# One core, one decoder trunk: the order of the attention passes, a scaling on ScalarE, and the layout of the token factors

## The chip, the core and the metric

The kernel runs on one core of one Trainium2 chip. The core has a matrix engine (TensorE: PE for its matmuls, PEld for its weight loads), VectorE (DVE), ScalarE (ACT), GpSimd (POOL) and SyncE (SP), which here only issues DMAs. Each engine works through its own list of instructions in the order in which the program has them; semaphores tie the lists together. Matmuls write to PSUM, which has eight banks of 128 partitions by 512 fp32 columns; SBUF holds everything else on the core.

The metric is the device time of one execution in microseconds.

## The reference: what is computed

The input is a residual stream of 512 tokens by 1024 columns, fp32. Two layers follow: a gated short convolution, then sliding-window attention whose keys and values are computed once. Each is followed by a SwiGLU feed-forward network (FFN) of width 2816.

```python
kv = rmsnorm(h, kv_norm) @ w_kv                       # 4 K heads, 4 V heads of 64
q = partial_rotary((rmsnorm(h, b_pre_norm) @ b_w_q))  # 16 heads of 64, blocks of 128 tokens
scores = q @ concat(k_prev_block, k_block).T / 8      # masked to a window of 128
probs = softmax(concat([scores, sink]))[..., :-1]     # the sink takes a share and gives nothing
h = h + rmsnorm((probs @ v) @ b_w_o, b_post_norm)
g, u = split(rmsnorm(h, ffn_pre_norm) @ w_gate_up)    # in each layer
h = h + rmsnorm((silu(g) * u) @ w_down, ffn_post_norm)
```

## The kernel before, in words

**Numbers.** A matrix product is made from a rounded part and a rest: every fp32 operand is split into `hi` (rounded to the format that TensorE reads fast, written by ACT) and `lo` (what is left, written by DVE), and `mm3` (L190 to L193) sums lo by hi, hi by hi and hi by lo. All transposes run on TensorE against an identity.

**FFN.** Each FFN has 11 pairs of gate and up tiles; one pair is computed plainly, the other ten as blocks of two by two with seven products in place of eight (`gate_jobs`). Three of the seven products (6, 7 and 4) go to the chain "X", which collects in a bank of 512 columns. For these, the token factor's hi and lo stand in one buffer, so that one matmul over 512 columns (L1048) multiplies hi and lo by the weights' hi at once, and a second over 256 columns (L1050) adds hi by the weights' lo. The other products use `mm3` over 256 columns. The token factors are made once per FFN in `factors` (L364): a buffer `two` of 1024 columns has hi in its first 512 columns and lo in the last 512, for two values of k. The operand of L1048 for one k therefore is two runs of 256 columns, 512 columns apart. Weights stream in by DMA; for each product DVE may first add two of them (L457), ACT writes their hi (L469) and DVE their lo (L470), three products ahead of TensorE. POOL's queue issues DMAs that form sums of weights in memory.

**Attention.** The 16 heads go in eight pairs, t = 0 to 7. A loop makes ten passes, i = 0 to 9, and the string `ORDER` (L47) gives the order in which a pass writes its steps into the engines' lists. The steps are, with their heads' place in the software pipeline:

- S0, S1 `scores` (pair i): 12 matmuls each over two banks `psc`, for tokens 0 to 255 and 256 to 511
- M0, M1 `maxima` (pair i, DVE, L1311): adds the mask, finds the maxima, and so frees the banks `psc`; E00 to E11 `exponents` (ACT, L1327)
- N0, N1 `normalise` (pair i, DVE, L1339 to L1344): sums, a reciprocal, and four scalings of the tiles `s`, one per head and block of 128 tokens; for N0 the first block's tile is 128x128, the other 128x256
- T0 to T3 `turn` (pair i-1, PE, L1356): transposes of `s` into banks `pt`, of which there are two; P0 to P3 `high` (ACT, L1369) and L0 to L3 `low` (DVE, L1373) split them and so free the bank for T two later
- W0 to W3 `weigh` (pair i-1, PE): by the values, into `po`; O- `out` splits `po` in the pass behind (ACT L1390, DVE L1391)
- Q0 to Q3 `project` (pair i+2, PE): the queries, in quarters of 6 matmuls, into `pq`; R- `rotate` (pair i+1, DVE L1237 and L1239, then POOL L1240 and L1241); H- `split` (pair i+1, ACT L1246, then POOL L1247), whose result S0 of the next pass reads; G the next weights of the queries (ACT L186, DVE L187)
- K, in pass 2 alone: the second half of the keys, on DVE, POOL and ACT as R- and H-
- g, Z, z, A: first parts of the output projection, from pass 4 on, and the first weights of the FFN behind

A line in an engine's list waits only for what it reads and for the buffer it writes; what stands behind it on that engine waits as well. The PSUM banks `pq`, `po` and `pe` rotate through four, `psc` and `pt` through two each.

Of the kernel before, what the change touches and what calls it, by code (L numbers as in the profile page):

```python
# [12 lines left out]
AF = mybir.ActivationFunctionType  # L13
ALU = mybir.AluOpType
# [4 lines left out]
S = 512  # L19
# [24 lines left out]
LINE_LEAD = 3  # L44

EARLY_IN, REST_IN = 2, 0
ORDER = (  # L47
    "R- T0 g0 S0 O- T1 Q0 M0 Q1 Z0 P0 P1 S1 T2 L0 Q2 L1 G M1 E00 E01 T3 H- Q3 P2 P3 E10 E11 Z1 z0 K W0 L2 L3 A A A N0 W1 W2 N1 W3 g1 z1"
)
STEP = {  # L50
    "S": "scores", "M": "maxima", "E": "exponents", "N": "normalise", "T": "turn", "P": "high",
# [4 lines left out]
EARLY = 4  # L56
# [16 lines left out]
def yoco_kernel(  # L73
# [22 lines left out]
    nc = tc.nc  # L96
# [15 lines left out]
    def name(s):  # L112
        uid[0] += 1
        return f"{s}_{uid[0]}"
# [4 lines left out]
    def wide(s, dt=F32):  # L119
        return wides.tile([P, D], dt, tag="wide", name=name(s))  # L120
# [52 lines left out]
    def split_weights(src, raw=None, slots=False):  # L173
        if raw is None:
            raw = fetch(src)
        if slots:
            hi, lo = Two("whi", F32R), Two("wlo", F32R)
            for h in range(2):
                c = slice(h * S, (h + 1) * S)
                nc.scalar.activation(hi[:, c], raw[:, c], AF.Copy)  # L180
                nc.vector.tensor_tensor(out=lo[:, c], in0=raw[:, c], in1=hi[:, c].bitcast(F32),
                                        op=ALU.subtract)
            return hi, lo
        hi = wsp.tile([P, D], F32R, tag="whi", name=name("whi"))
        lo = wsp.tile([P, D], F32R, tag="wlo", name=name("wlo"))
        nc.scalar.activation(hi, raw, AF.Copy)  # L186
        nc.vector.tensor_tensor(out=lo, in0=raw, in1=hi.bitcast(F32), op=ALU.subtract)  # L187
        return hi, lo
# [50 lines left out]
    class Update:  # L239
# [124 lines left out]
        def factors(self):  # L364


            x = self.x[0]
            made = {p: [] for p in range(1, 8)}
            for p, k0, c in ((1, 0, 0), (2, 4, 0), (3, 4, 256)):
                made[p] = [[a[:, c : c + 256] for a in x[k0 + k]] for k in range(4)]  # L370
            for j in range(2):
                q11, q21, q12, q22 = (self.parts[i, hf, j] for hf in range(2) for i in range(2))

                nc.vector.tensor_tensor(out=q11, in0=q11, in1=q12, op=ALU.subtract)
                nc.vector.tensor_tensor(out=q12, in0=q22, in1=q12, op=ALU.subtract)
                nc.vector.scalar_tensor_tensor(out=q22, in0=q22, scalar=-1.0, in1=q11,
                                               op0=ALU.mult, op1=ALU.subtract)
                nc.vector.scalar_tensor_tensor(out=q21, in0=q22, scalar=-1.0, in1=q21,
                                               op0=ALU.mult, op1=ALU.subtract)
                for p, q in ((6, q22), (5, q11), (7, q12), (4, q21)):  # L380
                    two = wide("xt", F32R)
                    hi, lo = two[:, :S], two[:, S:]
                    two = two.rearrange("p (i c) -> p i c", i=2)
                    nc.scalar.activation(hi, q, AF.Copy)
                    nc.vector.tensor_tensor(out=lo, in0=q, in1=hi.bitcast(F32),
                                            op=ALU.subtract)
                    made[p] += [[hi[:, c : c + 256], lo[:, c : c + 256], two[:, :, c : c + 256]]
                                for c in (0, 256)]
            return made

    class Ahead:
# [156 lines left out]
    for l in range(2):  # L548
# [3 lines left out]
        for rd, (f0, f1) in enumerate(ROUNDS[:-1]):  # L552
            k = slice(f0 // 2, f1 // 2)
# [106 lines left out]
    with tc.manual_schedule(engines=ALL):  # L660
# [294 lines left out]
    def ffn(l, before, ahead, gain, gpres, following):  # L955
# [5 lines left out]
        def gate_pair(pg, pu):  # L961
# [12 lines left out]
            return pair_sums(gr, acts[0])  # L974

        def gate_jobs(q, factors, out, to, then):


# [256 lines left out]
    def rope(ps, eng):  # L1235
        sh = slot("sh")
        nc.vector.stream_shuffle(sh, ps, swap)  # L1237
        a = slot("ra")
        nc.vector.tensor_tensor(out=a, in0=ps, in1=ctab, op=ALU.mult)  # L1239
        eng.tensor_tensor(out=sh, in0=sh, in1=stab, op=ALU.mult)  # L1240
        eng.tensor_tensor(out=a, in0=a, in1=sh, op=ALU.add)  # L1241
        return a

    def rope_split(a, eng):
        hi, lo = slot("rhi", F32R), slot("rlo", F32R)
        nc.scalar.activation(hi, a, AF.Copy)  # L1246
        eng.tensor_tensor(out=lo, in0=a, in1=hi.bitcast(F32), op=ALU.subtract)  # L1247
        return hi, lo
# [24 lines left out]
    class Heads:  # L1273
# [62 lines left out]
        def normalise(self, half):  # L1336
            se, rs = self.sums[half]
            pe = self.pe[half]
            nc.vector.tensor_tensor(out=se, in0=se, in1=rs, op=ALU.add)  # L1339
            rd = small.tile([P, 2, 2], F32, tag="rd", name=name("rd"))  # L1340
            nc.vector.reciprocal(out=rd, in_=se)
            for i, cc in self.spans(half):
                for e in range(2):
                    nc.vector.tensor_scalar(  # L1344
                        out=pe[e][:, cc], in0=pe[e][:, cc], scalar1=rd[:, e, i : i + 1],
                        scalar2=None, op0=ALU.mult,
                    )

        def turn(self, j):
            pt = bank("pt", ps_pt)  # L1350
# [67 lines left out]
    with tc.manual_schedule(engines=ALL):  # L1418
        last_tile(res, [[(0, 4)], [(0, 5)], [], [(0, 6), (0, 7), (1, 0), (1, 1)],
                        [(1, f) for f in (4, 5, 2, 3, 6, 7)]])  # L1420
        for hf in range(2):
            c = slice(hf * 256, (hf + 1) * 256)
# [48 lines left out]
    with tc.manual_schedule(engines=ALL):  # L1471
        sum_on("a0")
        for i in range(KT + 2):
            if i == KT:
                res = Update(mix_o, B_ATT, [G_FPRE[1]])
                res.leaves = True
                ahead = Ahead(first_weights(1))
            if i == KT + 1:
                res.load()
            for c in ORDER.split():  # L1480
                if c == "A":
                    if i == KT:
                        ahead.one()
                    continue
                if c == "K":
                    if i == 2:
                        ks.append(rope_split(rope(pk[1], nc.gpsimd), nc.gpsimd))
                    continue
                late = c.endswith("-")
                op, n = c[0], [int(d) for d in c[1:].rstrip("-")]  # L1490
                t = i - late
                if op == "g":

                    u = 2 * (t - EARLY - 1) + n[0]
                    if u in (-2, -1, 2, 3):
                        j = u + 2 if u < 0 else u
                        early_w.append(split_weights(w_o[j // 2, j % 2], slots=j >= EARLY_IN))
                    continue
                if op in "SMENTPLWO":
                    t -= op in "TPLWO"  # L1500
                    of = hp
                elif op in "QRH":
                    t += LEAD
                    of = qs
                elif op == "G":
                    t += LEAD + 1
                    of = qs
                    if KT <= t < KT + 4:
                        j = t - KT
                        rest_w.append(split_weights(w_o[j // 2, 2 + j % 2], slots=j >= REST_IN))  # L1510
                else:
                    t = 2 * (t - EARLY - 1) + n.pop(0)
                    of = early
                if 0 <= t < len(of) and not (op in "RH" and t < LEAD - 1):
                    getattr(of[t], STEP[op])(*n)
                if op in "RH" and i <= KT:
                    issue(len(issues) // 2 if op == "R" else len(issues))
            if i <= KT:
                sum_on(f"a{i + 1}")
        close(rest_w, at, EARLY, res, ahead, lambda: sum_on(f"a{KT + 2}"), 1)  # L1520
# [96 lines left out]
```

## Time and profile before

| What | Value |
|---|---|
| median of 3 runs | 1026.7 us (1026.5 to 1026.81) |
| profiled execution, own time | 1026.46 us |
| its span on the core | 1024.7 us |
| PE busy | 1015.1 us, 6168 matmuls |
| DVE busy | 858.7 us, 1440 instructions |
| ACT busy | 582.3 us, 1035 instructions |
| POOL busy | 196.9 us, 259 instructions |
| granted TensorE clock, mean | 0.999 |
| DMA | 244.52 MB, mean 239 GB/s |

The span holds, in this order, the convolution layer, the first FFN (its blocks of two by two run from 209.7 us), the attention passes (550.6 to 661 us), and the second FFN (blocks from 715 us). A row of a timeline has start, duration, engine, line, operation, output<-input, shape, and the count of equal instructions merged into the row. A duration of a matmul is from issue to modelled end and overlaps the next one; how long one holds the engine is read from the distance of two starts.

### The profile page before, as it was taken

The page shows a single profiled execution, that of the slowest core. Times are in us where ns is not written, and L with a number is a line of the kernel's source. Part 1 is how long each engine was busy: PE and PEld are TensorE (multiplying, and loading weights), DVE is VectorE, ACT ScalarE, POOL GpSimd, SP SyncE. Part 2 cuts the span into 40 slices and gives each one's busy share as a digit, 9 for nine tenths or more (in the row PEclk, how much of TensorE's full clock was granted, in tenths as well). Part 3 has the DMA queues.
Part 4 walks back from the last instruction along what each step waited for, and adds up shares of the span by engine and source line. Part 5 has one row for each costly group of instructions (what it writes and reads, how often), then busy time and mean ns, then how long its engine had stood idle before and what let it go on. Part 6 is the DMA issues. An engine that isn't in the chain of part 4 may idle for free.

```text
span 1024.7 us, 16538 instructions
## 1 busy us (share of the span) xinstructions
PE 1015.1 (99%) x6168; PEld 900.3 (88%) x6168; DVE 858.7 (84%) x1440; ACT 582.3 (57%) x1035; POOL 196.9 (19%) x259
## 2 busy tenths in 40 slices
PE   9999999999999999999999999999999999999997
PEld 8888888999889898998897888889998998989986
DVE  5766767889789988989869998778997898889896
ACT  7323445865655454666476776677666554645641
POOL 0443033112111111000123653232111010110001
PEclk9999999999999999999999999999999999999999
DMA  9897689459979699879504779976899576998742
GB/s 357 288 266 225 184 255 350 136 167 292 348 238 296 195 305 307 267 210 318 170 5 160 187 229 277 254 264 153 270 289 328 167 245 226 299 298 249 240 149 82
DMA packets 66576, 244.52 MB, mean 239 GB/s; under 512 B 7872, under 2 KB 8384, under 8 KB 54720
## 3 DMA queue, kind: packets, MB, share of 16 engines
q1 hardware_dynamic: 51328, 145.98, 38.9%
q0 software_dynamic: 14592, 96.48, 36.9%
q8 instruction: 48, 0.79, 0.3%
q10 hardware_dynamic: 576, 1.02, 0.3%
q14 instruction: 32, 0.26, 0.1%
HBM read 237.15 MB, written 102.76 MB: 332 GB/s over the span
## 4 chain that ended last, share of the span: by engine, by line
PE 85%; DVE 8%; ACT 2%; DMA 2%; issue 2%; POOL 0%; DVEq 0%; ACTq 0%
PE gx L1048 10%; PE gx L1050 5%; PE pcub L191 4%; PE pcub L192 4%; PE pcub L193 4%; PE gz L193 3%; PE gz L192 3%; PE gz L191 3%; PE px L191 3%; PE px L193 3%; PE px L192 3%; PE pmix L191 2%; PE pmix L192 2%; PE pmix L193 2%; DMA raw<-in_w_gb_dram 2%; PE gy L193 2%
## 5 line engine op out<-in xcount | busy, mean ns | idle before, releaser
L470 DVE TENSOR_TENSOR wlo<-raw,whi 128x1024 fp32r<-128x1024 f32 x225 | 274.8, 1227 | 64.5 <-ACT whi L469 64.1
L469 ACT ACTIVATE whi<-raw 128x1024 fp32r<-128x1024 f32 x225 | 234.0, 1051 | 104.8 <-DVE raw L457 22.3
L1048 PE MATMUL gx<-xt,whi 128*128 128x512 f32 x480 | 172.5, 399 | 0.1
L1050 PE MATMUL gx<-xt,wlo 128*128 128x256 f32 x480 | 135.0, 281 | 0.0
L1048 PEld LDWEIGHTS gx<-xt,whi 128*128 128x128 f32 x480 | 90.4, 188 | 19.7 <-DVE st L1008 0.3
L538 POOL DMA_DIRECT2D hsum<-in_w_gb_dram x96 | 63.7, 751 | 143.9 <-ACT whi L469 82.6
L1050 PEld LDWEIGHTS gx<-xt,wlo 128*128 128x128 f32 x480 | 90.9, 189 | 0.1
L1024 ACT ACTIVATE st<-gx 128x256 f32<-128x256 f32 x120 | 43.0, 379 | 63.1 <-PE gx L1050 47.8
L538 POOL DMA_DIRECT2D hsum<-hsum x32 | 25.3, 790 | 258.9 <-ACT whi L469 192.0
L1008 DVE TENSOR_TENSOR st<-gx,st 128x256 f32<-128x256 f32 x160 | 62.9, 420 | 4.3 <-ACT st L1024 2.9
L192 PE MATMUL pcub<-xhi,whi 128*128 128x512 f32 x168 | 65.4, 389 | 0.0
L191 PE MATMUL pcub<-xlo,whi 128*128 128x512 f32 x168 | 65.4, 389 | 0.0
L193 PE MATMUL pcub<-xhi,wlo 128*128 128x512 f32 x168 | 65.4, 389 | 0.0
L1062 ACT ACTIVATE gr<-gr 128x1024 f32<-128x1024 f32 x20 | 21.3, 1065 | 49.2 <-DVE gr L1008 49.2
L191 PE MATMUL px<-wlo,ahi 128*128 128x512 f32 x120 | 46.8, 390 | 0.1
L192 PE MATMUL px<-whi,ahi 128*128 128x512 f32 x120 | 46.7, 389 | 0.0
L193 PE MATMUL px<-whi,alo 128*128 128x512 f32 x120 | 46.7, 389 | 0.0
L193 PE MATMUL gz<-xhi,wlo 128*128 128x256 f32 x160 | 45.4, 284 | 0.0
L191 PE MATMUL gy<-xlo,whi 128*128 128x256 f32 x160 | 45.3, 283 | 0.0
L192 PE MATMUL gy<-xhi,whi 128*128 128x256 f32 x160 | 45.3, 283 | 0.0
L193 PE MATMUL gy<-xhi,wlo 128*128 128x256 f32 x160 | 45.3, 283 | 0.0
L192 PE MATMUL gx<-xhi,whi 128*128 128x256 f32 x160 | 45.3, 283 | 0.0
(265 smaller groups left out, 3064.5 us busy)
## 6 DMA issues: line engine op xcount, KB each, us to landing
hsum<-in_w_gb_dram POOLq DMA_DIRECT2D x96, 512.0 KB, 7.9
raw<-hsum SPq DMA_DIRECT2D x88, 512.0 KB, 7.6
raw<-in_w_gb_dram SPq DMA_DIRECT2D x60, 512.0 KB, 7.6
hsum<-in_w_dn_dram POOLq DMA_DIRECT2D x36, 512.0 KB, 8.8
raw<-in_w_dn_dram SPq DMA_DIRECT2D x32, 512.0 KB, 6.0
hsum<-hsum POOLq DMA_DIRECT2D x28, 512.0 KB, 5.9
raw<-in_w_in_dram SPq DMA_DIRECT2D x21, 512.0 KB, 7.8
hsum<-in_w_dn_dram POOLq DMA_DIRECT2D x12, 768.0 KB, 12.8
```

Of the source, the lines that this page charges most:

```text
L191: nc.tensor.matmul(out, whi, xlo, start=start, stop=False, **kw)
L192: nc.tensor.matmul(out, whi, xhi, start=False, stop=False, **kw)
L193: nc.tensor.matmul(out, wlo, xhi, start=False, stop=stop, **kw)
L469: self.begun = nc.scalar.activation(hi[:, :n], raw, AF.Copy)
L470: nc.vector.tensor_tensor(out=lo[:, :n], in0=raw, in1=hi[:, :n].bitcast(F32), op=ALU.subtract)
L538: nc.gpsimd.dma_start(dst, src, max_dma_last_dim=4 * 4 * S, **kw))
L1008: nc.vector.tensor_tensor(out=out, in0=a, in1=b, op=ALU.add)
L1024: nc.scalar.activation(ste, a, AF.Copy)
L1048: nc.tensor.matmul(banks[c][e], whi[:, kk], xboth[0], start=False, stop=False, **kw)
L1050: nc.tensor.matmul(banks[c][e][:, :256], wlo[:, kk], xhi, start=False, stop=k == 3 and p == 4, **kw)
L1062: nc.scalar.activation(kept[2], kept[2], AF.Silu)
```

## The change

Three things change.

In the attention loop the nine steps at the head of a pass now come from one of two strings: for passes 0 to 5, `HEAD`; from pass 6 on, `LOOP`. Against the former order, S0 is ahead of T0 in both. In HEAD, M0 is ahead of R-, of the weights g0 and of O- as well; in LOOP these keep their places. The rest of `ORDER` is as it was.

In `normalise`, for the first half (N0), the two scalings of 128x128 tiles (one per head) leave DVE for ACT.

In `factors`, hi and lo of one k now stand side by side: 256 columns of hi, 256 of lo. The operand of L1048 is one run of 512 columns; ACT and DVE write hi and lo in two runs of 256 each.

```diff
+HEAD, LOOP = "S0 T0 M0 R- g0 T1 O- Q0 Q1", "R- S0 T0 g0 T1 O- Q0 M0 Q1"
 ORDER = (
-    "R- T0 g0 S0 O- T1 Q0 M0 Q1 Z0 P0 P1 S1 T2 L0 Q2 L1 G M1 E00 E01 T3 H- ...
+    "Z0 P0 P1 S1 T2 L0 Q2 L1 G M1 E00 E01 T3 H- ...
 )
...
                 for p, q in ((6, q22), (5, q11), (7, q12), (4, q21)):
                     two = wide("xt", F32R)
-                    hi, lo = two[:, :S], two[:, S:]
-                    two = two.rearrange("p (i c) -> p i c", i=2)
+                    hi, lo = (two.rearrange("p (k i c) -> p k i c", k=2, i=2)[:, :, i]
+                              for i in range(2))
+                    q = q.rearrange("p (k c) -> p k c", k=2)
                     nc.scalar.activation(hi, q, AF.Copy)
                     nc.vector.tensor_tensor(out=lo, in0=q, in1=hi.bitcast(F32),
                                             op=ALU.subtract)
-                    made[p] += [[hi[:, c : c + 256], lo[:, c : c + 256], two[:, :, c : c + 256]]
-                                for c in (0, 256)]
+                    made[p] += [[two[:, c : c + 256], two[:, c + 256 : c + S],
+                                 two[:, c : c + S]] for c in (0, S)]
...
             for i, cc in self.spans(half):
                 for e in range(2):
-                    nc.vector.tensor_scalar(
-                        out=pe[e][:, cc], in0=pe[e][:, cc], scalar1=rd[:, e, i : i + 1],
-                        scalar2=None, op0=ALU.mult,
-                    )
+                    r = rd[:, e, i : i + 1]
+                    if half == i == 0:
+                        nc.scalar.activation(pe[e][:, cc], pe[e][:, cc], AF.Copy, scale=r)
+                    else:
+                        nc.vector.tensor_scalar(out=pe[e][:, cc], in0=pe[e][:, cc], scalar1=r,
+                                                scalar2=None, op0=ALU.mult)
...
-            for c in ORDER.split():
+            for c in ((HEAD if i <= EARLY + 1 else LOOP) + " " + ORDER).split():
```

What the first two make of the lists is shown at three places around the start of pass 3. Line numbers of the changed kernel are a few higher.

DVE, start of pass 3, before (behind N1's last scaling come R-, O- and M0; `sh` and `ra` are the rotation, `olo` is O-, the `ISA` rows on `psc` are M0, each followed by the row that stores its maximum):

```order
L1344 TENSOR_SCALAR s_6100<-s_6100,rd_6177 128x256
L1237 STREAM_SHUFFLE sh_6189<-pq_6041 128x512
L1239 TENSOR_TENSOR ra_6191<-pq_6041,ctab_5288 128x512
L1391 TENSOR_TENSOR olo_6218<-po_6148,ohi_6217 128x512
L1311 ISA s_6236,nm_6235<-psc_6203,mask,nsnk 128x128
L1311 ISA nm_6235 128x1
```

The same place now:

```order
L1350 TENSOR_SCALAR s_6100<-s_6100,rd_6177 128x256
L1313 ISA s_6211,nm_6210<-psc_6189,mask,nsnk 128x128
L1313 ISA nm_6210 128x1
L1313 ISA s_6212,nm_6210<-psc_6190,mask,nsnk 128x128
L1313 ISA nm_6210 128x1
L1313 ISA s_6211,nm_6210<-psc_6189,mask,nsnk 128x256
L1313 ISA nm_6210 128x1
L1313 ISA s_6212,nm_6210<-psc_6190,mask,nsnk 128x256
L1313 ISA nm_6210 128x1
L1239 STREAM_SHUFFLE sh_6217<-pq_6048 128x512
L1241 TENSOR_TENSOR ra_6219<-pq_6048,ctab_5288 128x512
L1395 TENSOR_TENSOR olo_6232<-po_6148,ohi_6231 128x512
```

M0 has moved ahead of R- and O-.

PE, start of pass 3, before (`po` is the last matmul of W3, `pt` is T0, `psc` is S0):

```order
L193 MATMUL po_6148<-lp_5619,vt_5610 128x256
L1356 MATMUL pt_6196<-ident,s_6049 128x128 x2
L1356 MATMUL pt_6196<-ident,s_6050 128x128 x2
L1299 MATMUL psc_6203<-rlo_5655,rhi_6116 128x256
L1299 MATMUL psc_6204<-rlo_5655,rhi_6116 128x256
```

Now (the rows show the end of S0, then T0 and T1; the first row of T0 reads the tile that ACT scales):

```order
L1301 MATMUL psc_6189<-rhi_5654,rlo_6117 128x256
L1301 MATMUL psc_6190<-rhi_5654,rlo_6117 128x256
L1360 MATMUL pt_6203<-ident,s_6024 128x128 x2
L1360 MATMUL pt_6203<-ident,s_6025 128x128 x2
L1360 MATMUL pt_6224<-ident,s_6024 128x128
L1360 MATMUL pt_6224<-ident,s_6099 128x128
L1360 MATMUL pt_6224<-ident,s_6025 128x128
L1360 MATMUL pt_6224<-ident,s_6100 128x128
L192 MATMUL pq_6235<-xlo_5322,whi_6094 128x512
```

S0's 12 matmuls have moved from between T0 and T1 to ahead of T0.

ACT, end of pass 2 and start of pass 3, before (`se` closes the exponents of pass 2, `rhi` belongs to K, `ohi` is O-, `phi` are P0 and P1):

```order
L1334 ACTIVATE se_6130<-nm_6098,snk 128x2 x2
L1246 ACTIVATE rhi_6144<-ra_6140 128x512
L1390 ACTIVATE ohi_6217<-po_6148 128x512
L1369 ACTIVATE phi_6201<-pt_6196 128x512
L1369 ACTIVATE phi_6226<-pt_6221 128x512
```

Now:

```order
L1336 ACTIVATE se_6130<-nm_6098,snk 128x2 x2
L1248 ACTIVATE rhi_6144<-ra_6140 128x512
L1348 ACTIVATE s_6024<-s_6024,rd_6158 128x128
L1348 ACTIVATE s_6025<-s_6025,rd_6158 128x128
L1394 ACTIVATE ohi_6231<-po_6148 128x512
L1373 ACTIVATE phi_6208<-pt_6203 128x512
L1373 ACTIVATE phi_6229<-pt_6224 128x512
```

The two rows L1348 are N0's scalings, which stand behind K's `rhi` and ahead of O-.

More of the change, by code (lines that the diff above doesn't have):

```diff
@@ L46 @@
 EARLY_IN, REST_IN = 2, 0
+HEAD, LOOP = "S0 T0 M0 R- g0 T1 O- Q0 Q1", "R- S0 T0 g0 T1 O- Q0 M0 Q1"
 ORDER = (
-    "R- T0 g0 S0 O- T1 Q0 M0 Q1 Z0 P0 P1 S1 T2 L0 Q2 L1 G M1 E00 E01 T3 H- Q3 P2 P3 E10 E11 Z1 z0 K W0 L2 L3 A A A N0 W1 W2 N1 W3 g1 z1"
+    "Z0 P0 P1 S1 T2 L0 Q2 L1 G M1 E00 E01 T3 H- Q3 P2 P3 E10 E11 Z1 z0 K W0 L2 L3 A A A N0 W1 W2 N1 W3 g1 z1"
 )
```

## The prediction

> **What bounds the kernel now.** I read the page's first part, then the chain that ended last, then busy time by stretches.
>
> ```profile
> PE 1015.1 (99%) x6168; PEld 900.3 (88%) x6168; DVE 858.7 (84%) x1440; ACT 582.3 (57%) x1035; POOL 196.9 (19%) x259
> PE 85%; DVE 8%; ACT 2%; DMA 2%; issue 2%; POOL 0%; DVEq 0%; ACTq 0%
> 550.00:610.00 60.00, 59.13 (x403) 48.41 (x404) 59.06 (x189) 43.28 (x136) 37.20 (x38) 1.00 0.71 189
> 715.00:995.00 280.00, 279.91 (x1769) 253.29 (x1769) 248.67 (x359) 159.22 (x232) 30.36 (x46) 1.00 0.79 253
> ```
>
> (The columns of a stretch are its length and the busy time of PE, PEld, DVE, ACT and POOL with counts, then granted clock, DMA share and GB/s.) TensorE bounds the kernel: in the 280 us of the second FFN's blocks it is idle for 0.09 us. Only in the attention passes 0 to 4 (550 to 610) are two engines full, PE with 59.13 and DVE with 59.06 of 60 us. So a gain must either shorten matmuls or take away waits of PE, and what loads DVE in those passes is what PE waits for.
>
> Busy time hides waits shorter than a matmul's modelled tail, so I take distances between starts. The change has one part for each of the two stages; I cost them apart.
>
> **The FFN part: the layout of the factors.** These rows show a row of plain 512-column matmuls, then eight pairs L1048 and L1050, then plain 256-column ones.
>
> ```profile
> 59.74 0.39 PE L191 MATMUL pcub<-xlo,whi 128*128 128x512 f32 x1
> ...
> 65.18 0.39 PE L191 MATMUL pcub<-xlo,whi 128*128 128x512 f32 x1
> 215.41 0.40 PE L1048 MATMUL gx<-xt,whi 128*128 128x512 f32 x1
> ...
> 218.24 0.28 PE L191 MATMUL gz<-xlo,whi 128*128 128x256 f32 x1
> ...
> 221.12 0.40 PE L1048 MATMUL gx<-xt,whi 128*128 128x512 f32 x1
> L1048 PE MATMUL gx<-xt,whi 128*128 128x512 f32 x480 | 172.5, 399 | 0.1
> L192 PE MATMUL pcub<-xhi,whi 128*128 128x512 f32 x168 | 65.4, 389 | 0.0
> ```
>
> From 59.74 to 65.18 there are 24 matmuls of 512 columns: 226.7 ns each. From 218.24 to 221.12 there are 24 of 256: 120.0 each. A pair should take 346.7 ns; the eight pairs from 215.41 to 218.24 take 2.83 us, 353.7 each. The excess is 7.0 ns a pair. What sets L1048 apart from the plain 512-column matmul is its moving operand in two runs, and that it alternates with 256 columns; the change takes away the first alone. No row has a 512-column operand in one run beside L1050, so I bound the gain: below 0 (the alternation costs it all; a loss I exclude, since one run is what all other 512-column matmuls read), above 10 ns (mean 399 against 389). I take 7.0: one more run is the plainer difference, and the weight loads alternate alike everywhere. With 480 pairs that is 3.4 us (bounds 0 and 4.8).
>
> Not all of it reaches the end:
>
> ```profile
> 389.37 18.78 DMA raw<-in_w_gb_dram
> 422.36 0.50 PE gx L1048
> 470.00:490.00 20.00, 19.98 (x91) 16.34 (x90) 19.70 (x28) 12.71 (x17) 0.00 (x0) 1.00 0.89 301
> 970.00:990.00 20.00, 19.98 (x103) 16.62 (x101) 19.64 (x30) 12.80 (x19) 0.00 (x0) 1.00 0.67 235
> ```
>
> In the chain of the first FFN a weight's DMA takes 18.78 us, and through it and DVE the chain gets back to PE at 422.36 only. About six of the ten blocks lie ahead of it: 6 x 24 x 7.0 ns = 1.0 us. If the landing is set by bandwidth this is lost, if by the issue it is kept; I count half, 0.5. In the last block of either FFN DVE is full (19.70 and 19.64 of 20), so the gain of two blocks, 2 x 24 x 7.0 = 0.3 us, turns into PE's wait for DVE. Left: 3.4 - 0.5 - 0.3 = 2.6 us.
>
> Making the factors in two runs of 256 adds no instruction; ACT's and DVE's 16 each may be a little longer. Their cover is the second half of the plain first pair's matmuls, which stand on PE ahead of the first product that reads them. I cost it at nothing; without this cover it would delay the first block of each FFN.
>
> **The attention part: where PE waits.** The step ahead of Q0 or S1 in each pass, as starts on PE:
>
> ```profile
> 558.06 0.39 PE L193 MATMUL pq<-xhi,wlo 128*128 128x512 f32 x1
> ...
> 560.72 0.48 PE L191 MATMUL pq<-xlo,whi 128*128 128x512 f32 x1
> ...
> 564.57 0.65 PE L1356 MATMUL pt<-ident,s 128*128 128x128 f32 x4
> ...
> 570.80 0.28 PE L193 MATMUL po<-lp,vt 128*128 128x256 f32 x1
> ...
> 572.77 0.48 PE L191 MATMUL pq<-xlo,whi 128*128 128x512 f32 x1
> ...
> 582.82 0.28 PE L193 MATMUL po<-lp,vt 128*128 128x256 f32 x1
> ...
> 585.44 0.48 PE L191 MATMUL pq<-xlo,whi 128*128 128x512 f32 x1
> ...
> 588.74 0.76 PE L1299 MATMUL psc<-rlo,rhi 64*128 64x256 f32 x2 [0.30 <-DVE nm L1311]
> ...
> 590.03 0.66 PE L1356 MATMUL pt<-ident,s 128*128 128x128 f32 x4
> ...
> 598.23 0.48 PE L191 MATMUL pq<-xlo,whi 128*128 128x512 f32 x1
> ...
> 602.79 0.66 PE L1356 MATMUL pt<-ident,s 128*128 128x128 f32 x4
> ...
> 647.68 0.28 PE L191 MATMUL po<-plo,vt 128*128 128x256 f32 x1
> ...
> 651.84 0.48 PE L191 MATMUL pe<-wlo,ohi 128*128 128x512 f32 x1
> ```
>
> From the last matmul of a pass to the next Q0 (T0, S0 and T1 between): pass 2 takes 572.77 - 570.80 = 1.97 us without a wait; pass 3 takes 2.62, so waits 0.65; pass 1 takes 2.66, of which 0.11 is the longer last matmul (226.7 against 120), so waits 0.58. From Q0 to T2 (Q0, Q1 and S1 between): pass 1 takes 3.85; pass 3 takes 4.59 and pass 4 takes 4.56, so they wait 0.74 and 0.71, S1 for the banks that M0 frees (row 588.74). In pass 8, 24 matmuls of 120 ns and eight transposes at about 0.11 should take 3.8; it takes 4.16, a wait of 0.4. All waits sum to 3.1 us: no reordering can give more here.
>
> What each becomes, with these rows of the other engines:
>
> ```profile
> 558.07 1.01 DVE L1344 TENSOR_SCALAR s<-s,rd 128x128 f32<-128x128 f32 x4
> 559.05 0.16 DVE L1339 TENSOR_TENSOR se<-se,rs 128x4 f32<-128x4 f32 x1
> ...
> 596.62 0.74 DVE L1237 STREAM_SHUFFLE sh<-pq 128x512 f32<-128x512 f32 x1
> ...
> 597.84 1.97 DVE L187 TENSOR_TENSOR wlo<-raw,whi 128x1024 fp32r<-128x1024 f32 x1
> ...
> 600.34 0.34 DVE L1311 CUSTOM_DVE_ANT_0 s<-psc,mask,nsnk 128x128 f32<-128x128 f32 x1
> ...
> 601.68 1.28 DVE L1373 TENSOR_TENSOR plo<-pt,phi 128x512 fp32r<-128x512 f32 x2
> 558.55 0.47 ACT L1334 ACTIVATE se<-nm,snk 128x2 f32<-128x2 f32 x2
> ...
> 562.51 0.39 ACT L1327 ACTIVATE s<-s,nm 128x128 f32<-128x128 f32 x1
> ...
> 582.89 0.63 ACT L1246 ACTIVATE rhi<-ra 128x512 fp32r<-128x512 f32 x1 [1.22 <-POOL ra L1241]
> 553.75 1.29 POOL L1241 TENSOR_TENSOR ra<-ra,sh 128x512 f32<-128x512 f32 x1
> ```
>
> Durations: M0 holds DVE from 600.34 to 601.68, 1.34 us; R- from 596.62 to 597.84, 1.22. N0's four scalings take 1.01 together (row 558.07); the two of 128 columns are the shorter half, some 0.4, which DVE saves in each of eight pairs. On ACT the price isn't in the trace; below it stands 0 (an idle ACT), above 0.39 each (the exponent of the same shape, 562.51). I take 0.25, nearer to that row: 0.5 us a pair, on an engine busy for 43.28 of 60 us. What counts is where these two wait in ACT's list: behind the last exponents, where DVE could scale earlier.
>
> - Pass 1, wait 0.58: R- in pass 0 comes M0's 1.34 us later. POOL's `ra` then ends at about 556.4 (now 553.75 + 1.29), ACT's H- waits for it, and the exponents E10 to E11 behind it end some 0.4 later, at 559.4 (now 559.0, row 558.55). N0's two scalings on ACT end at about 559.9; S0, now first, fills PE to 559.2. Q0 comes at about 560.6 against 560.72: gain 0.1.
> - Pass 3, wait 0.65: N0 on ACT stands behind K's `rhi`, which waits for POOL until 582.89, and ends at about 584.0. S0 (0.9 us) covers this from 582.95 on. Gain 0.5.
> - S1 of pass 3, wait 0.74: DVE does M0 as soon as N1 is done, at about 586.5; S1 is due at 588. Gain 0.74, all of it.
> - S1 of pass 4, wait 0.71: M0 passes R-, O- and also the weights g0 (1.97 us), so S1 no longer waits. But T2 behind it needs the bank `pt` that L0 frees, and L0 stands behind all of them in either order: from 596.62 to 602.3 are 5.7 us of DVE work. PE only changes its wait from S1 to T2. Gain 0.1.
> - Pass 8, wait 0.4: DVE reaches N1 0.4 earlier, for which T1 waited. Gain 0.2.
> - Passes 5 to 7 wait for nothing, so nothing is gained; S0 ahead of T0 only swaps two steps.
>
> Sum 1.6 us. The upper end is 3.1. For the lower end, H- late by 1.34 in each of six passes delays the splits P2 behind it on ACT; ACT idles about 1.0 us ahead of P3 in these passes, so 0.3 a pass is left, 6 x 0.3 = 1.8, with none of the gains: -1.8.
>
> ```profile
> 566.87 0.39 ACT L1369 ACTIVATE lp<-pt 128x256 fp32r<-128x256 f32 x1 [1.01 <-PE pt L1356]
> ```
>
> **The sum.** 2.6 + 1.6 = 4.2 us off the profiled execution's 1026.46 us (its span of 1024.7 and 1.8 around it): 1022.3. The median of the runs is 0.24 above this execution, so I forecast 1022.5.
>
> **Rivals.**
>
> - *The two runs are not the cause.* If the alternation of 512 and 256 columns costs the 7 ns, the FFN part gives 0, and the time is 1026.7 - 1.6 = 1025.1. For it: no row shows the pair in one run. Against it: a 256-column matmul ahead of an L1048 of another product takes 120 (218.24 to 221.12 holds one). The Trainium skill's page "SBUF — State Buffer" (in its section "Door 1: The DMA port swizzle") speaks for this rival: it says that SBUF is read in lines of 16 bytes and that an access pays when it crosses to a new one. Two runs of 256 fp32 cross as many lines as one of 512, so by that rule the layout is free and the time 1025.1; the rows' 7.0 ns are not explained by it, and I trust the rows. 14%.
> - *All waits go, and the whole matmul gain arrives.* 3.1 + 3.4 = 6.5: 1020.2. For it: DVE gets 0.4 us a pass; against it the count of L0's queue in pass 4. 14%.
> - *R- behind M0 becomes the bound (slower).* S0 is now first on PE in a pass, and needs the rotated queries, which come 1.34 us later through R-, POOL, H- and POOL. If S0 waits that whole time in passes 1 to 6, it costs 6 x 1.34 = 8.0 us, less the FFN's 2.6: 1032.1. It decides where POOL's `rlo` ends less than 1.34 us ahead of S0's due start:
>
> ```profile
> 556.12 1.31 POOL L1247 TENSOR_TENSOR rlo<-ra,rhi 128x512 fp32r<-128x512 f32 x1
> ...
> 565.34 1.58 POOL L1247 TENSOR_TENSOR rlo<-ra,rhi 128x512 fp32r<-128x512 f32 x1
> ```
>
>   For pass 1 it ended at 557.43, 0.9 ahead of PE's 558.3; there it is just reached. For pass 2 it ended at 566.92, 4.0 ahead of 570.9, which speaks against it. 8%.
>
> **Chances and range.** The forecast, with 1021 to 1024.2 as its own range, has 56%; the three rivals 14, 14 and 8; the remaining 8% are cases between, such as half the FFN gain beside a small loss in attention. A measurement of this kernel tells a change from none at about 0.2%, 2.05 us. Faster by more: 56 + 14, a third of the first rival (5) and 3 of the rest, 78%. Within: 9 of the first rival and 5 of the rest, 14%. Slower: 8%. For 8 times in 10 I go from 1020.0, below which half of the second rival lies, to 1026.0, above which the third and a few of the cases between lie.
>
> **What will show it.** The layout is right if L1048's mean falls from 399 to 389 ns and eight pairs take 2.77 us in place of 2.83; the first FFN's wait at 422 and DVE's full last blocks should then be a little longer. The attention part is right if S1 of pass 3 starts within 3.0 us of Q0, if the wait in pass 4 stands at T2 with L1373 as its releaser, and if the wait ahead of T0 in pass 1 names ACT. It is wrong if S0 waits for POOL's `rlo` beyond pass 1, if ACT's idle time ahead of P3 is gone and E10 comes later, or if L1048 stays at 399.

## The result and the profile after

The changed kernel takes 1028.68 us (median; 1027.74 to 1029.92) where the kernel before took 1026.5 on the same chip: a ratio of 1.0021, with an interval of 1.0013 to 1.0029. It was to take 1022.5, at most 1026.0. In a second comparison it took 1027.89 against 1026.18, 1.0016 (1.0007 to 1.0024). It is slower, by 1.7 to 2.2 us.

The head and the chain of the changed kernel's page look much as they did before:

```profile
PE 1013.6 (99%) x6168; PEld 899.5 (88%) x6168; DVE 858.8 (84%) x1424; ACT 586.3 (57%) x1051; POOL 196.6 (19%) x259
PE 90%; DVE 6%; ACT 2%; issue 1%; DMA 0%; POOL 0%; DVEq 0%; SPq 0%; ACTq 0%
```

DVE has 16 instructions less and is busy just as long (858.7 before). Between 550 and 661 us its sixteen scalings of 128 columns took 4.7 us; without them, the 48 of 256 columns went from 14.8 to 17.4 us, and the seven `wlo` of the queries' weights (L187, now L188) from 10.1 to 11.9.

Starts on PE tell where the time went. Both kernels have the same number of matmuls, so that the same place can be found in both: the first score matmul (`psc`), the first matmul of the output projection behind the passes (`pmix`), and the last matmul of all. Before:

```profile
550.61 0.38 PE L1299 MATMUL psc<-rlo,rhi 64*128 64x256 f32 x2
660.98 0.40 PE L191 MATMUL pmix<-wlo,ohi 128*128 128x512 f32 x1
1017.60 0.28 PE L193 MATMUL pmix<-whi,alo 128*128 128x256 f32 x1
```

Changed:

```profile
550.14 0.38 PE L1301 MATMUL psc<-rlo,rhi 64*128 64x256 f32 x2
662.29 0.40 PE L192 MATMUL pmix<-wlo,ohi 128*128 128x512 f32 x1
1018.91 0.28 PE L194 MATMUL pmix<-whi,alo 128*128 128x256 f32 x1
```

From `psc` to `pmix`, called the stretch below, it is 110.37 us before and 112.15 changed: all of the loss, 1.78 us, is there. Behind it, with the second FFN, both take 356.62. So the attention part lost where it should have gained 1.6 us, and the FFN part gave nothing where it should have given 2.6. In repeats the stretch agrees to some 0.1 us (112.13 for the changed kernel again; 110.28 to 110.29 in three kernels that leave attention as it was), while whole executions vary by 1 us and more (one spent 1.5 us more in the second FFN than the others). The experiments are therefore read by the stretch first.

**The FFN part.** The group of the wide matmul, and the ends of the first eight pairs:

```profile
L1050 PE MATMUL gx<-xt,whi 128*128 128x512 f32 x480 | 172.4, 399 | 0.0
215.37 0.40 PE L1050 MATMUL gx<-xt,whi 128*128 128x512 f32 x1
...
218.20 0.28 PE L192 MATMUL gz<-xlo,whi 128*128 128x256 f32 x1
```

With its operand in one run, the mean is still 399 ns, and the eight pairs still take 2.83 us.

**The attention part.** PE in passes 1, 3 and 4 of the changed kernel (idle time before a row, and what ended it, in brackets):

```profile
559.32 0.39 PE L1301 MATMUL psc<-rhi,rlo 64*128 64x256 f32 x2 [0.90 <-POOL rlo L1249]
...
560.25 1.17 PE L1360 MATMUL pt<-ident,s 128*128 128x128 f32 x8 [0.20 <-ACT s L1348]
561.18 0.47 PE L192 MATMUL pq<-xlo,whi 128*128 128x512 f32 x1
...
584.97 0.84 PE L1360 MATMUL pt<-ident,s 128*128 128x128 f32 x5 [0.28 <-ACT s L1348]
586.17 0.59 PE L1360 MATMUL pt<-ident,s 128*128 128x128 f32 x3 [0.36 <-DVE s L1350]
586.52 0.48 PE L192 MATMUL pq<-xlo,whi 128*128 128x512 f32 x1
...
590.73 0.66 PE L1360 MATMUL pt<-ident,s 128*128 128x128 f32 x4 [0.32 <-DVE plo L1377]
...
598.94 0.48 PE L192 MATMUL pq<-xlo,whi 128*128 128x512 f32 x1
...
604.08 0.66 PE L1360 MATMUL pt<-ident,s 128*128 128x128 f32 x4 [1.25 <-DVE plo L1377]
```

Counted from each kernel's first `psc`, Q0 of pass 1 (561.18; 560.72 before) comes 0.93 us later than before, Q0 of pass 3 (586.52) 1.55, T2 of pass 3 (590.73) 1.17, Q0 of pass 4 (598.94) 1.18, T2 of pass 4 (604.08) 1.76. So pass 1 loses 0.93, the way to Q0 of pass 3 loses 0.62 (0.2 of it in the last matmuls of pass 2, the rest at T0 and T1), S1 of pass 3 gains 0.38, and S1 and T2 of pass 4 lose 0.58.

Behind the first of these are rows of DVE and POOL in pass 0. Before, the rotation started on DVE at 551.56, and `wlo`, the step of G, stood behind M0. The last row is the same step in pass 1:

```profile
551.56 0.74 DVE L1237 STREAM_SHUFFLE sh<-pq 128x512 f32<-128x512 f32 x1
...
554.13 2.00 DVE L187 TENSOR_TENSOR wlo<-raw,whi 128x1024 fp32r<-128x1024 f32 x1
...
564.29 1.22 DVE L187 TENSOR_TENSOR wlo<-raw,whi 128x1024 fp32r<-128x1024 f32 x1
```

Changed:

```profile
552.51 0.74 DVE L1239 STREAM_SHUFFLE sh<-pq 128x512 f32<-128x512 f32 x1
...
553.73 2.02 DVE L188 TENSOR_TENSOR wlo<-raw,whi 128x1024 fp32r<-128x1024 f32 x1
553.38 1.29 POOL L1242 TENSOR_TENSOR sh<-sh,stab 128x512 f32<-128x512 f32 x1 [26.99 <-issue]
554.75 2.16 POOL L1243 TENSOR_TENSOR ra<-ra,sh 128x512 f32<-128x512 f32 x1
...
557.98 1.28 POOL L1249 TENSOR_TENSOR rlo<-ra,rhi 128x512 fp32r<-128x512 f32 x1
```

M0 puts R- off by 0.95 us by the clock, 1.42 counted from the first `psc`. Then comes what no step of the prediction had. `wlo`, which can take 1.22 us (row 564.29), takes 2.02 and ends at 555.75, 1.1 us after POOL's `sh` (554.67); and POOL's `ra`, 1.29 before, takes 2.16 and ends at 556.91, 1.2 us after `wlo`. Before, `wlo` was as long (row 554.13), but it was the later of the two: `ra` ran from 553.75 to 555.04, and `wlo` ended 1.1 us behind it, at 556.13. Now M0 no longer stands between R- and `wlo`, so `wlo` starts ahead of `ra`, and `ra` is the one that takes longer. That looks as if the two engines took turns; an experiment below tests it. S0's operand `rlo` ends at 559.26. Behind S0, T0 waits 0.20 us more for the scaling on ACT (row 560.25); the exponents ahead of that stand behind H-, and so behind `ra` as well.

### The profile page after: what moved, and what is told of

It is laid out like the page before. It is cut to its first block, busy times and chain, and to the rows that moved or that the text cites. A ratio compares the mean times of both kernels' runs of the same rounds, so it can differ in the third digit from the quotient of the medians.

```text
span 1026.0 us, 16537 instructions
## 1 busy us (share of the span) xinstructions
PE 1013.6 (99%) x6168; PEld 899.5 (88%) x6168; DVE 858.8 (84%) x1424; ACT 586.3 (57%) x1051; POOL 196.6 (19%) x259
## 4 chain that ended last, share of the span: by engine, by line
PE 90%; DVE 6%; ACT 2%; issue 1%; DMA 0%; POOL 0%; DVEq 0%; SPq 0%; ACTq 0%
PE gx L1050 11%; PE gx L1052 5%; PE pcub L192 4%; PE pcub L193 4%; PE pcub L194 4%; PE gz L194 4%; PE gz L193 4%; PE gz L192 4%; PE px L192 3%; PE px L194 3%; PE px L193 3%; PE pmix L193 2%; PE pmix L192 2%; PE pmix L194 2%; PE gy L194 2%; PE gy L193 2%
```

## The experiments

**The change in its parts.** The scaling alone:

```diff
+                    r = rd[:, e, i : i + 1]
+                    if half == i == 0:
+                        nc.scalar.activation(pe[e][:, cc], pe[e][:, cc], AF.Copy, scale=r)
```

> The kernel before with one part of the change: N0's two scalings of 128x128 tiles on ACT; order of the steps and layout of the factors as before. Theory A (the order of M0 and R- made the loss): the attention passes end within 0.5 us of before, S0 of pass 1 does not wait for POOL's rlo, and the waits ahead of T0 in passes 1 and 3 name ACT's scaling; time 1026 to 1027. Theory B (the scalings behind K's rhi and behind the exponents in ACT's list made the loss): the attention passes end 1 us or more later than before, time about 1027.5 to 1028.5.

1026.91 us against 1026.18, 1.0007 (0.9999 to 1.0016). The stretch is 110.83: 0.46 longer. T0 of pass 1 waits for the scaling behind the exponents in ACT's list (PE idle for 0.91 us), and T0 of pass 3 for 0.77, as theory A had it.

The order alone:

```diff
-            for c in ORDER.split():
+            for c in ((HEAD if i <= EARLY + 1 else LOOP) + " " + ORDER).split():
```

> The kernel before with the new order of the passes alone (HEAD in passes 0 to 5, LOOP behind); scalings on DVE, layout as before. Theory A (order): S0 of pass 1 waits about 1.0 us for POOL's rlo as in the changed kernel, T2 of pass 4 waits 1.2 us for L0, and the attention passes end 1.3 to 1.8 us later than before; time 1028 to 1028.7. Theory B (scaling on ACT): the passes end within 0.5 us of before or earlier; time 1025.5 to 1027.

```profile
560.38 0.38 PE L1300 MATMUL psc<-rhi,rlo 64*128 64x256 f32 x2 [0.90 <-POOL rlo L1248]
```

1028.0 against 1026.18, 1.0021 (1.0012 to 1.003); the stretch is 112.26. The order alone makes the whole loss, with S0's wait as in the changed kernel; theory A. The parts do not add up: with the new order the scaling on ACT costs nothing (112.15 with it).

The layout alone (the diff of `factors`):

> The kernel before with the new layout of the factors alone (hi and lo of one k side by side, one run of 512 columns). Theory A (the layout moves nothing on TensorE; the 7 ns a pair come from wide matmuls behind narrow ones): eight pairs take 2.83 us, the second FFN from the first matmul of the output projection is 356.6 us as before, time 1026.2 to 1026.8. Rival B (the forecast: the two runs cost 7.0 ns a pair, and something else in the changed kernel hid it): eight pairs take 2.77, the second FFN is 1.5 us shorter, time 1024.

```profile
215.65 0.40 PE L1049 MATMUL gx<-xt,whi 128*128 128x512 f32 x1
...
218.49 0.28 PE L191 MATMUL gz<-xlo,whi 128*128 128x256 f32 x1
```

1026.39 against 1026.54, 1.0 (0.9991 to 1.0009), and eight pairs take 2.84 us. A gain of 2.6 us lies outside this interval, and the pairs are as slow as before: the layout gives nothing, theory A.

The changed kernel once more:

> The changed kernel once more. Its profiled execution was 1.3 us longer in span than that of before, but the medians lie 2.2 us apart. If the other 0.9 us are a DMA of the first FFN that lands late in some executions, this profile's starts on PE run behind before's by up to 1 us already at the end of the first FFN; if they lie in attention, the shift there is above 1.75 us in this profile. Time 1028.2 to 1029.2.

1027.89, a stretch of 112.13, and PE 0.3 us ahead of before at the end of the first FFN. Neither place holds the other 0.9 us. This pair of medians lies 1.71 apart, which is the stretch's loss, so there may be no more to find; the interval of the first comparison holds 1.7 too.

**What the 7 ns a pair are.** The chain X grouped by width within a half:

```diff
-                                nc.tensor.matmul(banks[c][e][:, :256], wlo[:, kk], xhi, ...)
+                                if k == 3:
+                                    for j in range(4):
+                                        nc.tensor.matmul(banks[c][e][:, :256], wlo[:, jj], ...)
```

> The kernel before with the matmuls of the chain X of a block grouped by width: for each half first the four matmuls of 512 columns, then the four of 256, in place of four pairs; factors still in two runs. Theory A (the 7.0 ns a pair are the price of alternating widths): six of eight switches go, so eight matmuls take 1.39 us in place of 1.41 and the two FFNs shrink together by 0.75 x 480 x 7.0 ns = 2.5 us, up to 3.4 us if only the narrow matmul behind a wide one pays; time 1023 to 1024. Theory B (the two runs cost it after all, and the new layout has another cost of the same size): nothing changes, 1026.5. Theory C (a matmul of 512 columns costs 233.7 wherever its operand is a token factor): nothing changes either, and the eight rows stay at 1.41.

```profile
216.00 1.09 PE L1048 MATMUL gx<-xt,whi 128*128 128x512 f32 x4
...
218.81 0.28 PE L191 MATMUL gz<-xlo,whi 128*128 128x256 f32 x1
```

1025.23 against 1026.18, 0.9992 (0.9983 to 1.0001). Eight pairs take 2.81 us, so 2.5 of the 7.0 ns a pair go, not five. Then over both halves, eight wide and eight narrow:

> The kernel before with the products of the chain X written as eight matmuls of 512 columns and then eight of 256, over both halves. With four and four, eight pairs took 2.81 us in place of 2.83, and the 512-column matmuls behind narrow ones started 233 to 236 ns apart, the fourth 224 to 228. Theory A (the first few wide matmuls behind narrow ones are slow, then the row settles at 226.7): eight pairs take 2.79 to 2.80, and the FFNs lose another 60 x 0.015 = 0.9 us against four and four; time about 1024.3. Rival B (a wide matmul that writes a bank of the chain X is slow wherever it stands): all eight stay at 233 to 236, eight pairs take 2.81 to 2.83, no gain over four and four.

```profile
215.04 2.00 PE L1048 MATMUL gx<-xt,whi 128*128 128x512 f32 x8
216.88 1.12 PE L1053 MATMUL gx<-xt,wlo 128*128 128x256 f32 x8
217.83 0.28 PE L191 MATMUL gz<-xlo,whi 128*128 128x256 f32 x1
L1048 PE MATMUL gx<-xt,whi 128*128 128x512 f32 x480 | 120.2, 392 | 0.0
```

1024.34 against 1026.13, 0.9984 (0.9975 to 0.9992); eight pairs take 2.79. The starts inside the first row are 233, 236, 228, 233, 230, 227, 227 and 226 ns apart: the wide matmuls behind narrow ones are the slow ones, and from the sixth on they take the 226.7 of a plain row. A change to wide costs 26 ns in all, and the change back gives 6. Where wide and narrow alternate, every pair pays. That is theory A; why the first five are slow, no run shows.

**What the order costs.** Four orders of the steps at the head of a pass against the changed kernel's, all with the scaling on ACT and the new layout. LOOP in every pass (M0 behind R-, g0, O- and Q0 again, S0 still ahead of T0):

```diff
-            for c in ((HEAD if i <= EARLY + 1 else LOOP) + " " + ORDER).split():
+            for c in (LOOP + " " + ORDER).split():
```

> The changed kernel with LOOP at the head of every pass: S0 still stands ahead of T0 and the scalings of 128x128 on ACT, but M0 is behind R-, g0 and O- again. From the first score matmul to the first matmul of the output projection it was 110.37 us before, 112.15 changed, 110.83 with the scalings alone and 112.26 with the order alone. Theory A (M0 ahead of R- is the loss: S0 of pass 1 waits for a rotation that starts late on DVE and then meets DVE's weights on POOL): S0 of pass 1 waits less than 0.2 us, T2 of pass 4 has no wait of 1 us, and the stretch is 109.9 to 110.5; time 1026 to 1026.8. Rival B (S0 ahead of T0 is the loss, whatever M0 does): S0 of pass 1 waits 1 us again and the stretch is 111.5 or longer.

1025.96 against 1026.13, 0.9996 (0.9987 to 1.0005). The stretch is 109.98 and S0 of pass 1 does not wait: theory A. Then R- first in pass 0 alone (the edit below), and with it LOOP in pass 4:

```diff
+OPEN = "R- S0 T0 M0 g0 T1 O- Q0 Q1"
+            for c in ((OPEN if i == 0 else HEAD if i <= EARLY + 1 else LOOP) + " " + ORDER).split():
```

> The changed kernel with R- ahead of S0, T0 and M0 in pass 0 alone. Theory A (R- behind M0 in pass 0 costs the start of pass 1): the wait of 1.07 us at S0 of pass 1 goes and nothing else changes, so the stretch falls from 112.15 to about 111.1. Rival B (DVE is full in these passes, so that what pass 1 gains is waited for again at T0 or T2 of pass 1 or in pass 3): the stretch stays above 111.7.

> As the kernel with R- first in pass 0, and besides LOOP at the head of pass 4. Theory A (in pass 4, M0 first makes DVE wait 0.5 us for the scores while R- could run, and T2 pays for it through L0): the wait of 1.3 us at T2 of pass 4 goes, the 0.37 us at S1 come back, and the stretch is 0.5 us shorter than with R- first alone, about 110.6. Rival B (L0's queue of 5.7 us takes as long in either order): no difference of more than 0.2 us between the two.

The stretch falls to 110.75 (1.40 less than the changed kernel; more than the 1.1 expected) and to 110.46. The times are 1026.8, 1.0008 (0.9999 to 1.0017), and 1026.51, 1.0004 (0.9995 to 1.0013), against 1026.13. In pass 4 LOOP gives 0.29, not 0.5: the wait at T2 goes, and S1 waits longer than expected:

```profile
601.53 0.76 PE L1302 MATMUL psc<-rlo,rhi 64*128 64x256 f32 x2 [0.56 <-DVE nm L1314]
```

What M0 does there in the changed kernel is in its first row on DVE:

```profile
598.19 0.35 DVE L1313 CUSTOM_DVE_ANT_0 s<-psc,mask,nsnk 128x128 f32<-128x128 f32 x1 [0.51 <-PE psc L1301]
```

DVE, for whose `plo` PE waits later in the pass, is idle for 0.51 us until the scores are there, while R-, whose operand PE made in the pass before, stands behind M0. R- first, then M0, in all of the passes 0 to 5:

> The changed kernel with R- first in the passes 0 to 5 but M0 still ahead of g0 and O- (R- S0 T0 M0 g0 T1 O- Q0 Q1). Theory A (only R- behind M0 was harmful; M0 ahead of O- and g0 helps S1): S1 of pass 3 waits no longer and the stretch is 0.3 to 0.5 us shorter than with LOOP, 109.5 to 109.7. Rival B (DVE's whole list sets the time from pass 2 to 4, so that the wait only moves from S1 to T2): the stretch is 109.9 to 110.1 with the wait at T2.

```profile
589.32 0.66 PE L1361 MATMUL pt<-ident,s 128*128 128x128 f32 x4 [0.17 <-DVE plo L1378]
601.69 0.66 PE L1361 MATMUL pt<-ident,s 128*128 128x128 f32 x4 [0.27 <-DVE plo L1378]
```

1025.6 against 1026.47, 0.9991 (0.9982 to 1.0); the stretch is 109.53, 0.45 less than with LOOP. The waits do move from S1 to T2, as rival B said, but only 0.2 and 0.3 of them arrive there. M0 ahead of O- and g0 helps. This kernel differs from the changed one by the place of R- alone, and its stretch is 2.62 us shorter (109.53 against 112.15): R- behind M0 is what harms.

LOOP without the scaling on ACT:

> The kernel with LOOP in every pass and all scalings on DVE again. With the scaling on ACT the stretch was 109.98, before the change 110.37. Theory A (the scaling on ACT is what helps, by taking 0.6 us a pass off a full DVE, and S0 ahead of T0 covers its wait in ACT's list): the stretch is 110.3 or longer. Rival B (S0 ahead of T0 is what helps, and ACT only gives a wait at T0 of pass 3): the stretch is 109.9 or shorter.

1026.35 against 1026.47, 0.9997 (0.9989 to 1.0006); the stretch is 110.06, between the two theories and nearer to B. S0 ahead of T0 gives some 0.3 us; the scaling's 0.08 is no more than repeats differ by, so that it helps is not shown.

**The turns of DVE and POOL.** In pass 2 of the kernel with LOOP, the keys' rotation on POOL runs beside DVE's sums and scalings:

```profile
581.09 0.68 DVE L1377 TENSOR_TENSOR plo<-pt,phi 128x512 fp32r<-128x512 f32 x1
...
582.02 1.06 DVE L1341 TENSOR_TENSOR se<-se,rs 128x4 f32<-128x4 f32 x1
...
583.33 1.50 DVE L1350 TENSOR_SCALAR s<-s,rd 128x256 f32<-128x256 f32 x2
...
585.16 2.22 DVE L1350 TENSOR_SCALAR s<-s,rd 128x256 f32<-128x256 f32 x4
581.20 1.85 POOL L1242 TENSOR_TENSOR sh<-sh,stab 128x512 f32<-128x512 f32 x1
586.64 0.59 PE L1360 MATMUL pt<-ident,s 128*128 128x128 f32 x3 [0.37 <-DVE s L1350]
```

The sum over four columns takes 1.06 us, until `sh` has ended at 583.05. If these are turns, giving two of POOL's steps to DVE, which is full here, must end DVE's work sooner:

```diff
-                        ks.append(rope_split(rope(pk[1], nc.gpsimd), nc.gpsimd))
+                        ks.append(rope_split(rope(pk[1], nc.vector), nc.gpsimd))
```

> The kernel with LOOP in every pass, and the two POOL steps of K's rotation in pass 2 (sh and ra, 128x512) on DVE, which makes DVE's list longer by two steps of about 0.68 us. In the kernel with LOOP, DVE's sum of 128x4 ran 1.06 us beside POOL's sh instead of 0.16, a scaling 1.24 beside ra instead of 0.35, another 1.43 beside rlo; T1 of pass 3 waited 0.54 us. Theory A (DVE steps that read only SBUF wait until a POOL step beside them has ended): the 1.06 and the 1.24 return to 0.16 and 0.35, only one step beside rlo stays stretched, DVE's added 1.36 is paid back by 1.79, and the scores-to-projection stretch is 109.98 or up to 0.5 us less. Rival B (the stretched rows are only overlap in the records and DVE is simply full): the added 1.36 us come out at T1 of pass 3, which waits 1.5 us or more, and the stretch is 111 or longer.

```profile
581.98 0.16 DVE L1341 TENSOR_TENSOR se<-se,rs 128x4 f32<-128x4 f32 x1
...
582.38 1.66 DVE L1350 TENSOR_SCALAR s<-s,rd 128x256 f32<-128x256 f32 x2
...
584.36 1.14 DVE L1350 TENSOR_SCALAR s<-s,rd 128x256 f32<-128x256 f32 x4
582.45 1.43 POOL L1249 TENSOR_TENSOR rlo<-ra,rhi 128x512 fp32r<-128x512 f32 x1 [2.08 <-ACT rhi L1248]
```

1025.56 against 1026.47, 0.9988 (0.9979 to 0.9997); the stretch is 109.46, 0.52 less than with LOOP, and T1 of pass 3 waits no more. The 128x4 sum is back at 0.16, and one scaling is stretched, beside `rlo`. DVE has two steps more, and yet N1's four scalings end at 34.36 us from the first `psc`, where they ended at 34.89 with LOOP. Theory A. K's chain is shorter now as well, so that `rlo` is over (583.88) before those four start; how the 0.52 divide between that and the two POOL steps that are gone is not shown. The Trainium skill, "SBUF — State Buffer", section "SBUF: two separate sides", has this as a port pair which DVE and GpSimd hold by an exclusive lock for a whole instruction, and names DVE steps with two SBUF inputs among those that need it. These rows agree: `se` (two SBUF inputs) waits until `sh` has ended, while `plo` and the maxima, which read PSUM, keep their length beside POOL: 0.68 us beside the same `sh` (row 581.09), 0.47 beside the changed kernel's `ra` (a step of M1, at 555.67).

Last, the part of the collision in the loss of pass 1, with `wlo` behind M1 in pass 0:

```diff
+LATE_G = ORDER.replace("G M1", "M1 G")
```

> The changed kernel with G (the split of the next weights) behind M1 in pass 0 alone, so that DVE's step wlo no longer runs beside POOL's sh and ra of the rotation; M0 stays ahead of R-. In the changed kernel ra ran 2.16 us instead of 1.29 there, and S0 of pass 1 waited 1.07 us. Theory A (M0's 1.4 us alone would use up the slack and leave S0 a wait of 0.2; the other 0.87 are the collision): ra takes 1.29 us and S0 of pass 1 waits 0.1 to 0.4 us. Rival B (M0 ahead of R- is the whole loss): S0 still waits 0.9 us or more. The stretch may not follow, since DVE then waits for S1 ahead of M1: 111.2 to 112.2.

```profile
554.64 1.29 POOL L1244 TENSOR_TENSOR ra<-ra,sh 128x512 f32<-128x512 f32 x1
...
557.00 1.90 POOL L1250 TENSOR_TENSOR rlo<-ra,rhi 128x512 fp32r<-128x512 f32 x1
558.95 0.39 PE L1302 MATMUL psc<-rhi,rlo 64*128 64x256 f32 x2 [0.65 <-POOL rlo L1250]
```

`ra` is back at 1.29 us, but `wlo` now meets `rlo` (1.90), and S0 still waits, PE's idle time falling from 0.90 to 0.65. Neither theory's number: the collision moved. The time is 1028.2 against 1026.54, 1.0018 (1.0009 to 1.0027); the stretch is 111.92. How the 1.07 us divide exactly stays open. Counted from the first `psc`, the changed kernel's `rlo` ends 2.3 us later than before, 1.42 of it from M0 and 0.87 from the longer `ra`; some 1.2 of that was slack.

**Versions faster than both.** LOOP with the grouping of eight, and all that helped together (OPEN, K on DVE, the grouping), both with the scaling on ACT and the new layout:

> The changed kernel with LOOP in every pass, and the chain X as eight matmuls of 512 columns and eight of 256; the factors lie in one run of 512, where the kernel with the same grouping had two runs. Theory A (the layout costs and gives nothing): the eight pairs take 2.79 us as with two runs, the second FFN is as long as with two runs, and the two gains add: about 1.8 us from the grouping and 0.2 to 0.4 from the order and the scaling, time 1024.0 to 1024.4. Rival B (two runs do cost where wide matmuls follow each other): the 512-column rows fall to 226.7 and the second FFN is 0.5 us shorter than with two runs, time about 1023.3.

> All that helped, together: the changed kernel with R- first in the passes 0 to 5 and M0 behind S0 and T0, K's sh and ra on DVE, and the chain X as eight wide matmuls and eight narrow ones. If the gains add (0.84 us in the stretch from R- first and the scaling, about 0.4 more from K on DVE, 1.8 to 2.0 from the grouping): the stretch is 109.0 to 109.3 and the time 1023.2 to 1023.7. If R- first and K on DVE removed the same wait (T1 of pass 3): the stretch is 109.5 and the time 1023.7 to 1024.2.

The first takes 1023.91 against 1026.47, 0.9977 (0.9966 to 0.9988), a stretch of 109.97, and eight wide matmuls with the same distances as with two runs (234, 235, 229, 232, 231, 227): theory A, the layout gives nothing there either. The second takes 1023.3 against 1026.54, 0.997 (0.9959 to 0.9982), and its stretch is 109.02:

```profile
549.54 0.38 PE L1306 MATMUL psc<-rlo,rhi 64*128 64x256 f32 x2
658.56 0.40 PE L193 MATMUL pmix<-wlo,ohi 128*128 128x512 f32 x1
```

The gains add.

## Why the prediction was wrong

**The layout (2.6 us forecast, 0 measured).** The step that failed is the choice between the two things that set L1048 apart. I took the two runs and excluded the alternation on one row: a 256-column matmul ahead of an L1048 takes 120 ns. That row measured the narrow matmul, and the price falls on the wide ones behind it (1 to 9 ns on each of the first five in the row of eight). The first rival was right about this part (the layout is free, the alternation costs the 7 ns), and so was the rule that it drew from the Trainium skill's page "SBUF — State Buffer" ("Door 1: The DMA port swizzle"); that lines of 16 bytes are the reason, no run shows. The rest of the FFN part (what a late weight or a full last block takes back) had nothing to act on.

**Pass 1 (0.1 gained forecast, 0.93 lost).** R- did come M0's time later, and `ra` was reckoned to end at 556.4. It ended at 556.91 in an execution whose attention began 0.47 earlier, so at 557.38 by the clock of before, 1.0 late; and Q0 came at 561.65 by that clock where 560.6 was reckoned, 1.05 late. The step that failed is `ra`'s duration: 1.29 is what it takes alone, and the 0.87 over it are most of the error. The third rival, R- behind M0, named the place, S0 and POOL's `rlo`, with 0.9 us of slack that "is just reached"; but it had the wait in six passes or not at all, and it came in one. Its chance of 8% was too small because the price of a later R- was taken from one row, without asking what would then run beside it.

**Pass 3 (0.5 and 0.74 gained forecast; 0.62 lost, 0.38 gained).** N0 on ACT was to end at 584.0, behind K's `rhi`, and M0 to start at 586.5. Measured:

```profile
583.99 0.63 ACT L1248 ACTIVATE rhi<-ra 128x512 fp32r<-128x512 f32 x1 [1.86 <-POOL ra L1243]
584.53 0.68 ACT L1348 ACTIVATE s<-s,rd 128x128 f32<-128x128 f32 x2
584.69 2.21 DVE L1350 TENSOR_SCALAR s<-s,rd 128x256 f32<-128x256 f32 x4
584.70 1.27 POOL L1249 TENSOR_TENSOR rlo<-ra,rhi 128x512 fp32r<-128x512 f32 x1 [0.74 <-ACT rhi L1248]
```

The step that failed is that K's `rhi` was left where it stood before. Counted from the first `psc` it starts 1.57 us later (PE itself is only 0.92 late at Q0 of pass 2), and the scaling behind it ends at 585.21. With R- first in pass 0 alone T0 still waits 0.28 for the scaling; with R- first in all six passes it does not, so this wait comes from R- behind M0 in the passes between. N1's four take 2.21 beside `rlo` (1.85 before); with K on DVE the same four took 1.14 (row 584.36 above). M0 starts at 586.83, so S1 waits no more, but T0 and T1 wait instead and T2 takes 0.4 over.

**Pass 4 (0.1 gained forecast, 0.58 lost).** "5.7 us of DVE work in either order" was right as a sum of work and wrong as a time: put first, M0 must wait for PE.

**The rest.** The scaling on ACT was taken at 0.25 us each; two take 0.68 together, so 0.34 each. S0 ahead of T0 can give more than the 0.1 us set down for pass 1: with M0 in its old place and all scalings on DVE it hides T0's wait there, and Q0 comes 9.60 us after the first `psc` instead of 10.11. Pass 8 gained nothing of 0.2 (4.15 us against 4.16). The three signs that were to show the attention part right all came true: S1 of pass 3 starts 2.92 us after Q0, the wait in pass 4 stands at T2 with `plo` as its releaser, and T0 of pass 1 names ACT. They say where a wait stands, not how long it is.

**What the trace of before already told.** I quoted `wlo` with 1.97 us at 597.84 and took that for its price. The same trace has it with 1.22 (row 564.29) and with 2.00 in the very place that decided pass 1 (row 554.13). I quoted `se` with 0.16 at 559.05; in pass 2 the trace has it with 1.05 (at 580.47). I did not ask why one step has two durations. The answer, a POOL step beside the longer one, is what decided pass 1 and a part of pass 3.

## What to carry to other kernels

When one instruction form has two durations in a trace, find what ran beside the longer one before moving it; here DVE and POOL take turns on steps that read only SBUF, and an order that looked free in each engine's own list put a turn of 0.87 us on the path. A step whose operands are there goes ahead of one that must wait for the engine that bounds the kernel. Where matmuls of two widths can be grouped, group them: alternating them cost 7 ns a pair here, and the layout of the operand nothing.

## What was not expected of the hardware

Behind 256-column matmuls, the first five of a row of 512-column ones start their successors 228 to 236 ns later, before the distance settles at 226.7; alternating pairs pay 7.0 ns each, 480 of them 3.4 us. Grouping by eight brought the pair from 353.7 to some 349 ns and 1.8 us of the whole. And a 128x4 sum on DVE took 1.06 us in place of 0.16 because it started beside a POOL step.
